# The feed-forward residual and the second activation tile change places, the first output units go by halves, and pads move the small products

## The chip, the cores and the metric

The kernel runs on one core of one Trainium2 chip. The metric is the device time of one execution in microseconds (us); lower is better. Five engines work side by side: TensorE multiplies matrices (PE in the rows), VectorE (DVE), ScalarE (ACT) and GpSimd (POOL) do everything element by element, and SyncE (SP) issues most DMA transfers. Each engine works through its own queue in order and waits on semaphores for the others.

## The reference

One decoder layer on x of 256 positions by 2048 channels, in float32. Two branches run side by side on the normalised x, are weighted by sigmoid gates, added and projected; a convolutional feed-forward block follows. Cut to its core:

```python
h = rmsnorm(x, attn_w)
z, xbc, dt, q, k, v, gates = split(h @ w_in)          # the input projection, in parts
y_ssm  = ssd_mixer(z, xbc, dt, ...) @ w_ssm_out       # 8 groups of 8 heads
y_attn = moba_attention(q, k, v, ...) @ w_attn_out    # 16 heads of 128, with a position bias
g_s, g_a = split(sigmoid(gates + b_gate))
x = x + (g_s * y_ssm + g_a * y_attn) @ w_out
u = causal_dwconv(rmsnorm(x, ffn_w) @ w_up)           # 2 x 5632 channels, 3 taps
out = x + (silu(u[:half]) * u[half:]) @ w_down
```

Inside `ssd_mixer` each group of 512 channels is normalised by the mean of its squares (`yg * rsqrt(mean(yg * yg) + EPS)`). The position bias of a head is a table of 32 buckets, looked up by distance.

## The kernel before

**Tiling.** Activations lie with channels on the 128 partitions and the 256 positions along them. A float32 product is made of three in the rounded format f32r: each operand is split into a high part and a rest, and high x high, high x rest and rest x high are summed. Weights come in units of 1 MB: `unit` loads one into `wraw` (SyncE's queue, three buffers), ScalarE copies each half to `whi` (L181), VectorE forms the rest `wlo` (L182), three buffers each. `cm_chunk` then makes the matmuls of a half: eight pairs of `whi` with high part and rest (L196, L197), eight of `wlo` with the high part (L199), 24 matmuls of 256 columns; a unit has 48. The weights are the stationary operand there, the activations the moving one. In `tm_chunk` (L325, L326, L331: V, Q and K) it is the other way, with 512 columns.

**Stages in time.** V until 126 us; Q, K and attention until 307, then gate and attention output (`hp` and `ot` as moving tiles) until 492; the SSD groups with their input projections (`hn`) and output units (`yt`) until 1246; `w_out` (`mt`) until 1342; the feed-forward block as up and down projections in thirds (`fh` up, `a` down: up 0, up 1, down 0, up 2, down 1, down 2) to the end. The second third's down projection stands at 1908.7 to 2000.8.

**Order.** A scheduler fixes each engine's queue from the order in which the code is written. Attention and SSD steps are lists that `sp.tick()` deals out between the weight units, one step a tick; the steps of an SSD group end with ydot(3), norm1 (squares), norm1b (`all_sum`: split the sum of squares into `nsp`, add over partitions by one matmul with `onesr`, L249) and norm2. In `merge`, each of 16 tiles of the last SSD output units is multiplied by its gate (`gs`) and added to the attention part (`ma`), both loaded by GpSimd (L807, L808), with VectorE's L809 to L811; L812 and L813 write its high part and rest to `mt`, which `w_out` reads.

**Where tiles lie.** The base pool holds the three 32 KB slots of tag s32, `whi`, `wlo` and `wraw`, and stage pools follow behind it. A tile's byte offset in a partition follows from the sizes ahead of it. Offsets modulo 128 in the built program:

| operands of TensorE | offsets before |
|---|---|
| tiles in s32 slots: hp, ot, hn, yt, mt, fh, first and third activation tile | 0 |
| whi, wlo | 64 |
| second activation tile a2 (pool of the feed-forward block) | 64 |
| qh, ql and kh, kl (scores) | 0 and 0 |
| pth, ptl and vt (probabilities by values) | 0 and 0 |
| bch, bcl: first half stationary, second half moving | 96 and 96 |
| xh, xl and mh, ml (ydot) | 96 and 96 |
| nsp, ssp and onesr | 96 and 0 |

## Time and profile before

| | |
|---|---|
| time, median of three runs | 2066.89 us (2066.75 to 2069.88) |
| the profiled execution: time, span | 2071.27 us, 2069.5 us |
| mean granted clock of TensorE | 0.999 of full speed |
| busy: TensorE, VectorE, ScalarE, GpSimd | 99%, 70%, 55%, 3% |
| DMA, mean over the span | 197 GB/s |

The terms of a sum are made from the profiled execution and then set against the median. In rows, a name such as `mm<-hn,whi` reads output, then inputs; a time in square brackets is the idle time before the instruction, with what ended it. Matmuls are pipelined: one of 256 columns is shown as 0.28 us long, while the next starts 0.11 to 0.12 us after it.

### The profile page before, as it was taken

The page shows a single profiled execution, that of the slowest core. Times are in us where ns is not written, and L with a number is a line of the kernel's source. Part 1 is how long each engine was busy: PE and PEld are TensorE (multiplying, and loading weights), DVE is VectorE, ACT ScalarE, POOL GpSimd, SP SyncE. Part 2 cuts the span into 40 slices and gives each one's busy share as a digit, 9 for nine tenths or more (in the row PEclk, how much of TensorE's full clock was granted, in tenths as well). Part 3 has the DMA queues.
Part 4 walks back from the last instruction along what each step waited for, and adds up shares of the span by engine and source line. Part 5 has one row for each costly group of instructions (what it writes and reads, how often), then busy time and mean ns, then how long its engine had stood idle before and what let it go on. Part 6 is the DMA issues. An engine that isn't in the chain of part 4 may idle for free.

```text
span 2069.5 us, 39670 instructions
## 1 busy us (share of the span) xinstructions
PE 2053.5 (99%) x16594; PEld 1995.0 (96%) x16594; DVE 1457.4 (70%) x2324; ACT 1146.9 (55%) x1565; POOL 62.7 (3%) x119
## 2 busy tenths in 40 slices
PE   8999999999999999999999999999999999999999
PEld 7888889999999999999999999999999999999999
DVE  6567777456678787787888786677777765677444
ACT  6456556444557756656566654565555553455333
POOL 0000000000000000000000120000000000000000
PEclk9999999999999999999999999999999999999999
DMA  7654446555555555555555666555555555555555
GB/s 275 249 189 154 172 173 215 195 203 194 205 194 203 195 195 190 178 203 194 186 199 187 217 238 233 190 184 199 189 199 189 200 188 201 187 201 188 183 177 170
DMA packets 65892, 407.45 MB, mean 197 GB/s; under 512 B 8405, under 2 KB 10469, under 8 KB 22192
## 3 DMA queue, kind: packets, MB, share of 16 engines
q1 hardware_dynamic: 55152, 376.45, 51.7%
q0 software_dynamic: 7104, 22.17, 3.4%
q10 hardware_dynamic: 3456, 6.29, 0.9%
q8 instruction: 130, 2.13, 0.4%
q14 instruction: 50, 0.41, 0.1%
HBM read 398.50 MB, written 9.53 MB: 197 GB/s over the span
## 4 chain that ended last, share of the span: by engine, by line
PE 95%; DVE 1%; issue 1%; DMA 1%; ACT 1%; POOL 0%; SPq 0%; POOLq 0%; DVEq 0%
PE mm L197 26%; PE mm L196 26%; PE mm L199 26%; PE mm L325 4%; PE mm L331 4%; PE mm L326 4%; PE cc L210 1%; PE cc L209 1%; PE cc L211 1%; DVE wlo L182 1%; DMA g<-gs 1%; PE cc L418 0%; PE cc L666 0%; DMA g<-ma 0%; DMA wraw<-wv 0%
## 5 line engine op out<-in xcount | busy, mean ns | idle before, releaser
L181 ACT ACTIVATE whi<-wraw 128x1024 fp32r<-128x1024 f32 (+2 forms) x728 | 756.1, 1041 | 767.0 <-PE mm L197 632.6
L182 DVE TENSOR_TENSOR wlo<-wraw,whi 128x1024 fp32r<-128x1024 f32 (+2 forms) x728 | 870.0, 1197 | 313.4 <-ACT whi L181 308.4
L196 PE MATMUL mm<-hn,whi 128*128 128x256 f32 x1536 | 359.7, 277 | 0.0
L197 PE MATMUL mm<-hn,whi 128*128 128x256 f32 x1536 | 358.9, 276 | 0.0
L197 PE MATMUL mm<-fh,whi 128*128 128x256 f32 x1408 | 328.0, 276 | 0.0
L196 PE MATMUL mm<-fh,whi 128*128 128x256 f32 x1408 | 328.0, 276 | 0.0
L196 PEld LDWEIGHTS mm<-hn,whi 128*128 128x128 f32 x1536 | 288.6, 188 | 0.1
L197 PEld LDWEIGHTS mm<-hn,whi 128*128 128x128 f32 x1536 | 288.4, 188 | 0.0
L196 PEld LDWEIGHTS mm<-fh,whi 128*128 128x128 f32 x1408 | 264.3, 188 | 0.0
L197 PEld LDWEIGHTS mm<-fh,whi 128*128 128x128 f32 x1408 | 264.3, 188 | 0.0
L199 PE MATMUL mm<-hn,wlo 128*128 128x256 f32 x1536 | 205.9, 276 | 0.0
L199 PEld LDWEIGHTS mm<-hn,wlo 128*128 128x128 f32 x1536 | 188.6, 188 | 0.0
L199 PE MATMUL mm<-fh,wlo 128*128 128x256 f32 x1408 | 188.3, 276 | 0.0
L199 PEld LDWEIGHTS mm<-fh,wlo 128*128 128x128 f32 x1408 | 172.7, 188 | 0.0
L197 PE MATMUL mm<-a,whi 128*128 128x256 f32 x704 | 167.5, 279 | 0.0
L196 PE MATMUL mm<-a,whi 128*128 128x256 f32 x704 | 167.5, 279 | 0.0
L325 PE MATMUL mm<-whi,hp 128*128 128x512 f32 x384 | 153.6, 400 | 6.8 <-ACT whi L181 6.7
L326 PE MATMUL mm<-whi,hp 128*128 128x512 f32 x384 | 151.8, 395 | 0.0
L197 PEld LDWEIGHTS mm<-a,whi 128*128 128x128 f32 x704 | 133.2, 189 | 0.0
L196 PEld LDWEIGHTS mm<-a,whi 128*128 128x128 f32 x704 | 133.2, 189 | 0.0
L196 PE MATMUL mm<-yt,whi 128*128 128x256 f32 x512 | 119.3, 276 | 0.0
L197 PE MATMUL mm<-yt,whi 128*128 128x256 f32 x512 | 119.3, 276 | 0.0
(290 smaller groups left out, 3182.0 us busy)
## 6 DMA issues: line engine op xcount, KB each, us to landing
wraw<-wup SPq DMA_DIRECT2D x88, 1024.0 KB, 4.8
wraw<-wssd SPq DMA_DIRECT2D x80, 1024.0 KB, 4.8
wraw<-wqk SPq DMA_DIRECT2D x32, 1024.0 KB, 4.8
wraw<-wso SPq DMA_DIRECT2D x32, 1024.0 KB, 4.9
wraw<-wd SPq DMA_DIRECT2D x32, 1024.0 KB, 4.8
wraw<-wga SPq DMA_DIRECT2D x16, 1024.0 KB, 4.9
wraw<-wao SPq DMA_DIRECT2D x16, 1024.0 KB, 5.0
wraw<-wgs SPq DMA_DIRECT2D x16, 1024.0 KB, 4.8
```

The costliest lines, as they stand in the source:

```text
L181: S.activation(hi[:, i:i + m], raw[:, s], AF.Copy)
L182: V.tensor_tensor(lo[:, i:i + m], raw[:, s], hi[:, i:i + m].bitcast(F32), op=SUB)
L196: PE.matmul(ps, w, xh[:, k0 + k], start=first and k == 0, stop=False)
L197: PE.matmul(ps, w, xl[:, k0 + k], start=False, stop=False)
L199: PE.matmul(ps, lo[:, k * 128:(k + 1) * 128], xh[:, k0 + k], start=False, stop=last and k == nk - 1)
L209: PE.matmul(ps, ah, bh, start=first, stop=False)
L210: PE.matmul(ps, ah, bl, start=False, stop=False)
L211: PE.matmul(ps, al, bh, start=False, stop=last)
L325: PE.matmul(pst[tt], hph[:, k0 + k, ts], wh, start=first and k == 0, stop=False)
L326: PE.matmul(pst[tt], hpl[:, k0 + k, ts], wh, start=False, stop=False)
L331: PE.matmul(pst[tt], hph[:, k0 + k, ts], wl, start=False, stop=last and k == 1)
```

## The change

The residual `x1` moves from an s32 slot to a tile of its own in the feed-forward pool, and the second activation tile, which stood in that pool, to the slot; the third activation tile takes the first one's. The first two `w_out` units are multiplied by halves: first half of unit 0, first half of unit 1, second half of 0, second half of 1. The split of the sum of squares moves into the step of ydot(3) and the squares, an empty step follows, and the matmul comes in norm1b as before. The fp32 bias product becomes two f32r products, for which ScalarE and VectorE split the table `rel` and VectorE casts the one-hot table `oh`. Pads (`pad2` to `pad4`, and 16 columns in `bch` and `bcl`) shift tiles.

```diff
@@ -242,9 +242,15 @@
 
 
     def all_sum(pool, v, out, name, **kw):
+        sum_out(sum_split(pool, v, name, **kw), out)
+
+    def sum_split(pool, v, name, **kw):
         t = pool.tile([128, 2, T], F32R, name=name, **kw)
         S.activation(t[:, 0], v, AF.Copy)
         V.tensor_tensor(t[:, 1], v, t[:, 0].bitcast(F32), op=SUB)
+        return t
+
+    def sum_out(t, out):
         ps = c_tile()
         PE.matmul(ps.rearrange("p (a t) -> p a t", t=T), onesr, t, start=True, stop=True)
         S.activation(out, ps[:, T:], AF.Copy)
@@ -306,8 +312,14 @@
         oh = ap.tile([REL_BUCKETS + 1, 384], F32, name="oh")
         nc.gpsimd.dma_start(rel, d["rel"])
         nc.gpsimd.dma_start(oh, d["onehot"])
+        ohr = ap.tile([REL_BUCKETS + 1, 384], F32R, name="ohr")
+        rels = ap.tile([REL_BUCKETS + 1, 2, H], F32R, name="rels")
+        V.tensor_copy(ohr, oh)
+        S.activation(rels[:, 0], rel, AF.Copy)
+        V.tensor_tensor(rels[:, 1], rel, rels[:, 0].bitcast(F32), op=SUB)
         pb = c_tile()
-        PE.matmul(pb[:H, :384], rel, oh, start=True, stop=True)
+        PE.matmul(pb[:H, :384], rels[:, 0], ohr, start=True, stop=False)
+        PE.matmul(pb[:H, :384], rels[:, 1], ohr, start=False, stop=True)
         rows = ap.tile([H, 384], F32, name="brows")
         V.tensor_copy(rows, pb[:H, :384])
         nc.gpsimd.dma_start(brow, rows)
@@ -377,6 +389,7 @@
 
     _, oh_, ol_ = r32("ot")
     pts = []
+    ap.tile([128, 16], F32, name="pad3")
     for i in range(2):
         pth = ap.tile([128, 512], F32R, name=f"pth{i}")
         ptl = ap.tile([128, 512], F32R, name=f"ptl{i}")
@@ -416,6 +429,8 @@
                 for h in range(2):
                     for tt in range(2):
                         PE.transpose(ps[:, h * 256 + tt * 128:h * 256 + (tt + 1) * 128], n[:, tt, 2 * (j % 2) + h], ident)
+                if j == 0 and key == "k":
+                    ap.tile([128, 16], F32, name="pad4")
                 hi = ap.tile([128, 512], F32R, name=key + "h", bufs=1)
                 lo = ap.tile([128, 512], F32R, name=key + "l", bufs=1)
                 S.activation(hi, ps, AF.Copy, scale=w)
@@ -639,8 +654,8 @@
             last = S.activation(pr, pr, AF.Silu)
             with tc.issue_after(last.ins):
                 S.preload_act_table_set(LN_EXP)
-            bh = sd.tile([128, 2, T], F32R, name="bch")
-            bl = sd.tile([128, 2, T], F32R, name="bcl")
+            bh = sd.tile([128, 2, T + 16], F32R, name="bch")[:, :, :T]
+            bl = sd.tile([128, 2, T + 16], F32R, name="bcl")[:, :, :T]
             S.activation(bh, pr[:, 8:10], AF.Copy)
             V.tensor_tensor(bl, pr[:, 8:10], bh.bitcast(F32), op=SUB)
             st["b"] = (bh, bl)
@@ -699,6 +714,8 @@
                 m1 = m[:, 512:768].rearrange("p (h t) -> p h t", t=128)
                 V.tensor_tensor(m0, m0, st["cb"][:, None, 0:256].to_broadcast([128, 2, 256]), op=MUL)
                 V.tensor_tensor(m1, m1, st["cb"][:, None, 256:384].to_broadcast([128, 2, 128]), op=MUL)
+                if g == 0 and p == 0:
+                    sd.tile([128, 16], F32, name="pad2")
                 mh = sd.tile([128, 768], F32R, name="mh", bufs=2)
                 ml = sd.tile([128, 768], F32R, name="ml", bufs=2)
                 S.activation(mh, m, AF.Copy)
@@ -729,11 +746,11 @@
             S.activation(sq2, yz[:, 2:4], AF.Square)
             V.tensor_tensor(sqt, sqt, sq2, op=ADD)
             V.tensor_tensor(sqt[:, 0], sqt[:, 0], sqt[:, 1], op=ADD)
-            st["sq"] = sqt
+            st["sq"] = sum_split(sd, sqt[:, 0], "nsp", tag="cb")
 
         def norm1b():
             w = sd.tile([128, 3, T], F32, name="nw", tag="m", bufs=2)
-            all_sum(sd, st["sq"][:, 0], w[:, 0], "nsp", tag="cb")
+            sum_out(st["sq"], w[:, 0])
             V.tensor_scalar(w[:, 0], w[:, 0], 1.0 / 512, EPS, op0=MUL, op1=ADD)
             st["r"] = rsq_in(w[:, 0], w[:, 1], w[:, 2])
 
@@ -747,8 +764,8 @@
             S.activation(yh, yz, AF.Copy)
             V.tensor_tensor(yt[:, b, 1, o:o + 4], yz, yh.bitcast(F32), op=SUB)
 
-        steps = [silu, [bc, xtr(0), xtr(1)], dec(0), dec(1), ydot(0), dec(2), ydot(1), dec(3), ydot(2), ydot(3),
-                 norm1, norm1b, norm2]
+        steps = [silu, [bc, xtr(0), xtr(1)], dec(0), dec(1), ydot(0), dec(2), ydot(1), dec(3), ydot(2), [ydot(3), norm1],
+                 [], norm1b, norm2]
         return steps
 
     def out_unit(q, u, done):
@@ -819,14 +836,22 @@
 
     fctx = contextlib.ExitStack()
     fp = fctx.enter_context(tc.tile_pool(name="ffn", bufs=1))
-    x1f = xs_slot("x1")
-    x1 = x1f[:, :KT * T].rearrange("p (k t) -> p k t", t=T)
+    x1 = fp.tile([128, KT, T], F32, name="x1")
     for c in range(4):
         S.dma_start(x1[:, 4 * c:4 * c + 4], d["xT"][:, 4 * c:4 * c + 4])
     _, fh, fl = r32("fh")
     ssum = fp.tile([128, T], F32, name="ssum")
-    for o in range(KT):
-        ps = cm_unit(d["wout"][o], mh_, ml_)
+
+    def out_products():
+        parts = [unit(d["wout"][o]) for o in range(2)]
+        pss = [mm_tile()[:, :T] for _ in range(2)]
+        for c in range(2):
+            for o in range(2):
+                cm_chunk(pss[o], parts[o][c], mh_, ml_, 8 * c, 8, c == 0, c == 1)
+        for o in range(KT):
+            yield o, pss[o] if o < 2 else cm_unit(d["wout"][o], mh_, ml_)
+
+    for o, ps in out_products():
         V.tensor_tensor(x1[:, o], ps, x1[:, o], op=ADD)
         S.activation(fh[:, o], x1[:, o], AF.Copy, scale=sm("ffn_w", o))
         V.scalar_tensor_tensor(fl[:, o], x1[:, o], sm("ffn_w", o), fh[:, o].bitcast(F32), op0=MUL, op1=SUB)
@@ -847,8 +872,8 @@
 
     def up(th):
         f0, n = thirds[th]
-        if th == 1:
-            at = fp.tile([128, 2, 16, T], F32R, name="a2")
+        if th == 2:
+            at = acts[0]
         else:
             at = base.tile([128, 2, 16, T], F32R, name=f"a{th}", tag="s32", bufs=3)
         for i in range(n):
```

Offsets modulo 128 that differ in the built program: second activation tile 0 (weights still 64), qh and ql 64 (kh, kl 0), pth and ptl 64 (vt 0), bch and bcl 96 stationary and 32 moving, mh and ml 32 (xh, xl 96). The other operands of the table keep theirs.

On TensorE, at the start of `w_out`, last rests of the halves; `mm` is the output unit, `wlo` the half. Before:

```order
L199 MATMUL mm_14256<-mt_13610,wlo_14249 128x256 x8
...
L199 MATMUL mm_14256<-mt_13610,wlo_14253 128x256 x8
...
L199 MATMUL mm_14319<-mt_13610,wlo_14312 128x256 x8
...
L199 MATMUL mm_14319<-mt_13610,wlo_14316 128x256 x8
L196 MATMUL mm_14384<-mt_13610,whi_14376 128x256
```

With the change:

```order
L199 MATMUL mm_14275<-mt_13619,wlo_14258 128x256 x8
...
L199 MATMUL mm_14276<-mt_13619,wlo_14268 128x256 x8
...
L199 MATMUL mm_14275<-mt_13619,wlo_14262 128x256 x8
...
L199 MATMUL mm_14276<-mt_13619,wlo_14272 128x256 x8
L196 MATMUL mm_14393<-mt_13619,whi_14385 128x256
```

The second unit's first half now stands ahead of the first unit's second half, the first that reads late tiles of `mt`; units from the third on stand as before.

On VectorE, at the end of the merge (`slotA` is the sum, `g` the gates and the merged tile). Before:

```order
L811 TENSOR_TENSOR g<-slotA,g 128x256
L809 TENSOR_TENSOR slotA<-mm,slotA 128x256
L182 TENSOR_TENSOR wlo<-wraw,whi 128x1024
L813 TENSOR_TENSOR mt<-g,mt 128x256
L810 TENSOR_TENSOR slotA<-slotA,g 128x256
L811 TENSOR_TENSOR g<-slotA,g 128x256
L813 TENSOR_TENSOR mt<-g,mt 128x256
L830 TENSOR_TENSOR x_14239<-mm,x_14239 128x256
```

With the change (L826, L827, L828 and L830 are what L809, L810, L811 and L813 were; L855 is the addition to x):

```order
L828 TENSOR_TENSOR g<-slotA,g 128x256
L826 TENSOR_TENSOR slotA<-mm,slotA 128x256
L182 TENSOR_TENSOR wlo<-wraw,whi 128x1024
L830 TENSOR_TENSOR mt<-g,mt 128x256
L827 TENSOR_TENSOR slotA<-slotA,g 128x256
L828 TENSOR_TENSOR g<-slotA,g 128x256
L182 TENSOR_TENSOR wlo<-wraw,whi 128x1024
L830 TENSOR_TENSOR mt<-g,mt 128x256
L182 TENSOR_TENSOR wlo<-wraw,whi 128x1024
```

One more weight rest stands ahead of the last tile's rest, and one behind it; the weight rest behind the first gate addition shown is still behind it.

On ScalarE, at the end of SSD group 0 (`pre` and silu are group 1's, `sqt` the squares, L774 a gate of the SSD branch). Before:

```order
L639 ACTIVATE pre_4836<-pre_4836 128x2560
L774 ACT_TABLE_LOAD
L774 ACTIVATE g<-mm,small 128x256
L729 ACTIVATE sqt_6346<-slotA 128x512
L181 ACTIVATE whi<-wraw 128x1024 x2
L246 ACTIVATE nsp<-sqt_6345 128x256
```

With the change:

```order
L654 ACTIVATE pre_4844<-pre_4844 128x2560
L746 ACTIVATE sqt_6293<-slotA 128x512
L791 ACT_TABLE_LOAD
L791 ACTIVATE g<-mm,small 128x256
L249 ACTIVATE nsp<-sqt_6292 128x256
L181 ACTIVATE whi<-wraw 128x1024 x3
```

The squares go ahead of the table load and the gate, and the copy into `nsp` ahead of two weight halves. On VectorE the rest of `nsp` follows the sum of the squares in the same way, and on TensorE the matmul with `onesr` stands eleven matmuls earlier in groups 0 and 1, in the same place in groups 2 and 3.

## Rows read from the trace of the kernel before

**Rows 1.** The page: busy time of each engine, share of the span, instructions.

```profile
PE 2053.5 (99%) x16594; PEld 1995.0 (96%) x16594; DVE 1457.4 (70%) x2324; ACT 1146.9 (55%) x1565; POOL 62.7 (3%) x119
```

**Rows 2.** Stretches: us, TensorE busy (count), granted clock, DMA share, GB/s.

```profile
62.00:125.00 63.00, 63.00 (x277) 1.00 0.67 245
334.20:518.70 184.50, 184.50 (x1569) 1.00 0.59 208
520.00:545.00 25.00, 25.00 (x223) 1.00 0.69 240
1255.40:1258.60 3.20, 3.20 (x17) 0.50 0.78 275
1259.00:1343.00 84.00, 84.00 (x716) 1.00 0.55 194
1691.20:1777.00 85.80, 85.80 (x759) 1.00 0.54 196
1910.00:2000.00 90.00, 90.00 (x752) 1.00 0.50 176
```

**Rows 3.** Timeline of TensorE, end of attention: start, busy us, line, operands.

```profile
333.39 0.28 PE L209 MATMUL cc<-pth,vt 128*128 128x256 f32 x1
...
333.99 0.28 PE L211 MATMUL cc<-pth,vt 128*128 128x256 f32 x1
```

**Rows 4.** Waits of TensorE: total us, times, longest.

```profile
PE cc L249 <- DVE nsp L247: 2.8, 4, 0.7
```

**Rows 5.** Timeline of TensorE around nsp, group 0.

```profile
622.84 0.28 PE L196 MATMUL mm<-hn,whi 128*128 128x256 f32 x1
...
624.94 0.47 PE L249 MATMUL cc<-nsp,onesr 128*128 128x512 f32 x1 [0.69 <-DVE nsp L247]
625.25 0.28 PE L197 MATMUL mm<-hn,whi 128*128 128x256 f32 x1
```

**Rows 6.** Timeline of ScalarE ahead of it.

```profile
620.38 0.62 ACT L729 ACTIVATE sqt<-slotA 128x512 f32<-128x512 f32 x1
...
622.80 0.41 ACT L246 ACTIVATE nsp<-sqt 128x256 fp32r<-128x256 f32 x1
```

**Rows 7.** Timeline of VectorE ahead of it.

```profile
624.38 0.42 DVE L247 TENSOR_TENSOR nsp<-sqt,nsp 128x256 fp32r<-128x256 f32 x1
```

**Rows 8.** Timeline of TensorE, start of the output projection.

```profile
1250.25 0.28 PE L197 MATMUL mm<-mt,whi 128*128 128x256 f32 x1
1251.59 0.38 PE L196 MATMUL mm<-mt,whi 128*128 128x256 f32 x1 [1.06 <-ACT mt L812]
1252.94 0.38 PE L197 MATMUL mm<-mt,whi 128*128 128x256 f32 x1 [0.97 <-DVE mt L813]
1254.18 0.38 PE L196 MATMUL mm<-mt,whi 128*128 128x256 f32 x1 [0.86 <-ACT mt L812]
...
1258.87 0.28 PE L197 MATMUL mm<-mt,whi 128*128 128x256 f32 x1
```

**Rows 9.** Timeline of VectorE, end of the merge.

```profile
1250.66 0.42 DVE L811 TENSOR_TENSOR g<-slotA,g 128x256 f32<-128x256 f32 x1 [1.51 <-DMA g<-ma]
...
1251.34 1.21 DVE L182 TENSOR_TENSOR wlo<-wraw,whi 128x1024 fp32r<-128x1024 f32 x1
```

**Rows 10.** Timeline of GpSimd: issues of the one-hot table and of the attention gate.

```profile
2.00 0.54 POOL L308 DMA_DIRECT2D oh<-onehot  x1
...
1243.87 0.54 POOL L808 DMA_DIRECT2D g<-ma  x1 [0.74 <-DVE slotA L810]
```

**Rows 11.** The page's DMA issues: count, KB each, median us to landing.

```profile
g<-ma POOLq DMA_DIRECT2D x16, 128.0 KB, 4.4
...
oh<-onehot POOLq DMA_DIRECT2D x1, 49.5 KB, 4.3
```

**Rows 12.** Timeline of TensorE, bias product.

```profile
60.10 0.81 PE L310 MATMUL cc<-oh,rel 33*16 33x384 f32 x2
```

**Rows 13.** Timeline of VectorE, first hp rests.

```profile
4.70 0.88 DVE L256 SCALAR_TENSOR_TENSOR hp<-xt,aw,hp 128x256 fp32r<-128x256 f32 x2 [4.70 <-ACT hp L255]
```

## The prediction

> **What bounds the kernel now.** I read the busy table first: TensorE is busy for 2053.5 of 2069.5 us [rows 1]. The waits of TensorE come next: past the one ahead of the first matmul they are a handful, so removing waits alone can give little. The third view cuts the busy time by stage [rows 2], and that is where this change can act. The count of a stretch takes in two matmuls that lap over its ends, so the starts are the count less two, and the stretch divided by them is the **step** from one matmul to the next. All matmuls of 256 columns do the same work, and yet the step has three values at full clock: 113.1 and 113.3 ns in the SSD stage (25.00 us / 221) and for the first activation tile (85.80 / 757), 117.7 and 117.6 ns in the gates and the attention output (184.50 / 1567) and in the output projection (84.00 / 714), and 120.0 ns for the second activation tile a2 (90.00 / 750). The reader is to see that a busy TensorE is not the same as a fast one: between the levels lie 4.5 and 6.7 ns for every matmul.
>
> What separates the levels I read by laying addresses beside steps. Where the two operands of a matmul lie at the same byte offset modulo 128 (a2 and its weights, both 64), the step is 120.0. The products of probabilities and values (both 0) step by (333.99 - 333.39) / 5 = 0.120 us too [rows 3]. Where they differ by 64 (all activation tiles of the base slots, 0, against weights at 64) it is 113 or 117.7. The level 117.7 has no operands of its own: it holds for tiles that elsewhere run at 113, is there from 334.2 on, right behind those products, and lasts through ot, hp and hn; hn's matmuls alone, from 520 on, are at 113.1 again. I read it as a slower phase that a stretch of same-offset matmuls or a stall leaves behind, and that lasts until something resets it. The 120.0 is shown directly; the phase is my inference.
>
> **The change part by part**, against the profiled 2071.3 us (span 2069.5).
>
> *a) Second activation tile in a base slot.* Its offset goes from 64 to 0, against weights at 64, as the first tile has it. Sixteen units of 48 matmuls = 768, by 120.0 - 113.3 = 6.7 ns: **-5.1 us**. Lower gain: if the tile lands in the 117.7 phase, 768 x 2.3 ns = 1.8. The exchange costs nothing else: x, now in the pool, is no operand of TensorE; the last third takes up the first tile's memory again, which the down projection before it has finished reading.
>
> *b) The pads in the attention stage.* They move pth/ptl to 64 (vt stays 0) and qh/ql to 64 (kh/kl stay 0). Their 192 matmuls of 256 columns lose 192 x 6.7 ns = 1.3 us directly. The 512-column units between them may sit in the same phase: seven groups of 24 after such products, by some 4 ns (an estimate, from the 4.5 above), is 0.7. With the hidden-state units at the end of the stage 2.2; bounds 0.5 and 3.5: **-2.2**. If no same-offset products stand before 334.2, the phase isn't entered there and 1567 matmuls return to 113.2: 1567 x 4.5 ns = **-7.0**; if it is entered for another reason, 0.
>
> *c) The pads in the SSD stage.* bch/bcl now pair 96 with 32, mh/ml 32 with xh/xl 96. These are 96 + 48 matmuls of 256 columns by at most 6.7 ns and 96 of 512, which I bound by the same: 0 to 1.6, taken as **-1.0**. This is below the middle of what 192 such matmuls cost in b) because the stream runs at 113.1 around them.
>
> *d) Group norm.* Four waits of TensorE for nsp, 2.8 us in all [rows 4]; each costs more than its idle time, since the matmul before it and after it drain and refill: in group 0 it starts 624.94 - 622.84 = 2.10 us after the chunk's first matmul, where the eleven ahead of it need 11 x 0.113 = 1.25, and the next follows 0.31 later where a 512-column step is 63.00 us / 275 = 0.229 [rows 2, 5]. So 0.85 + 0.08 = 0.93, four times 3.7. Now nsp's copy and rest stand in the step of the squares: on ScalarE the squares go ahead of a table load and a gate that stood ahead of them, so all three end where the squares end today, 620.38 + 0.62 = 621.00; the copy follows at once, 0.41 [rows 6], and on VectorE the rest, 0.42 [rows 7]: ready at about 621.9. Its matmul moves eleven earlier, to the start of the chunk at 622.84 [rows 5]: 0.9 us of slack. Behind the copy on ScalarE the next weight halves come some 0.4 us later, and no wait of TensorE for them exists around here to grow. **-3.7**, bounds 2 and 3.7.
>
> *e) First output units by halves.* TensorE runs dry here because the last two merged tiles, high part and rest, come late: waits until 1251.59, 1252.94 and 1254.18, then 15 matmuls in 3.20 us (213 ns) at granted clock 0.50, that is the lower level, 1.2 GHz [rows 2, 8]. The 26 matmuls between 1250.25 and 1258.87 took 8.6 us where 26 x 113.3 ns = 2.95 would do; 5.7 are lost. The cause is a transfer: VectorE's addition waits 1.51 us for the attention gate until 1250.66 [rows 9]; issued at 1243.87 [rows 10], it took 6.8 us against a median of 4.4 [rows 11]. Now TensorE does both units' first halves first, which need no late tile: 48 matmuls from 1246.29, done by 1251.7. But the second unit's first half needs its wlo from VectorE, which stands behind that very addition: at 1251.34 + 1.21 = 1252.55 it is there, while its matmuls are due at 1250.82. The wait is not gone, it **moved**: at most 1.7 us, and 0.15 when the transfer takes its usual time. The last tile's rest now stands behind one more wlo, at about 1255.1, 0.15 late at most. Units one and two end at about 1258.8 instead of 1263.0: **-4.2**. What follows, some 700 matmuls at 117.6, entered the phase by the stall at the lower clock; with one stall of 1.7 us in place of three and no lower clock I expect 113: 700 x 4.4 ns = **-3.1**, else 0. x's transfer is issued earlier on ScalarE's queue, between two weight halves, and waits for nothing recent: 0.
>
> *f) Bias product.* Two passes in fp32, busy 0.81 us [rows 12], become two of 384 columns; at 0.229 for 512, 0.17 each: **-0.4**.
>
> *g) The start.* The split of rel and the cast of the one-hot table now stand first on VectorE. The table is issued at 2.00 [rows 10] and lands 4.3 us later [rows 11], so the first hp rest comes at about 7.2 instead of 4.70 + 0.44 [rows 13], just where TensorE wants it, 7.25. Everything on VectorE behind it, the first wlo too, waits along. The weights' arrival paces TensorE there. **+0.1**, bounds 0 and 0.4.
>
> Sum: -5.1 - 2.2 - 7.0 - 1.0 - 3.7 - 4.2 - 3.1 - 0.4 + 0.1 = **-26.6**, hence 2044.7 profiled. The profiled execution stands 4.4 us above the median of 2066.9 (runs to 2069.9); part of that may be the same late transfer, so I take 25 off the median: **2042**, main band 2037 to 2046.
>
> **The rivals.** *R1, the phase stays* from 334 to 519: something else than the same-offset products starts it. For it: it also begins behind the stalls after 1251 [rows 2, 8]. Against: the products right ahead of its start step by 120 [rows 3]. b) gives 7.0 less: **2049**. With e)'s phase staying as well, 2052.
>
> *R2, placement does nothing:* the steps differ for what runs beside the matmuls, not for addresses. Then only d), e) without the phase, f) and g) remain: 8.2 of 2066.9, **2059**. Against it: the second tile's matmuls are the same as the first's, beside less traffic (DMA share 0.50 against 0.54 [rows 2]), and slower. The Trainium skill would side with R2: its page "SBUF — State Buffer", section "Who interferes with whom", gives TensorE two independent read ports for moving operand and weights and says that it never waits on anyone; the trace speaks against that, with 120.0 and 113.3 ns for the same shapes.
>
> *R3, slower:* the small products at their new offsets leave the phase behind in the SSD stage, which today is free of it: mh with xh at equal offsets are followed by 113.1 [rows 2]. From 519 to 1246 there are some 6,400 matmuls: 6,400 x 4.5 ns = 28.4 us back, and if the gates' 7.0 isn't won either, 2042 + 35.4 = **2077**. It decides from where 25 us are lost: without the gates' 7.0, when 4,000 of the 6,400 run at 117.6. Against it: a2 shows the price of equal offsets, and no long stretch with a difference of 64 that begins from 113 leaves it by itself.
>
> **How the numbers follow.** Forecast 0.63; R1 (with or without the output projection) 0.15; R2 0.08; R3 0.06; partial mixtures between 2052 and 2066 0.08. The range 2036 to 2054 holds the first two and the lower mixtures. What can be told from no change here is about 0.2%, 4.1 us: faster (below 2062.8) takes all but R3 and a little of the mixtures, 0.91; R3 where it is partial ends within, 0.04; slower 0.05.
>
> **What would show it.** Right: the second tile's stretch at 113.3 per step; 334 to 487 at 113; no wait for nsp; one wait for wlo of at most 1.7 us in the second output unit's first half and a granted clock of 1.00 there; the stretch behind it at 113. Wrong: 117.6 in the SSD stage or in the gates, or a2's successor at 120.0, which would refute the reading by offsets. A longer start would show in the first wait of hp's rest.

## The result

The changed kernel takes 2054.61 us (median of four runs, 2052.70 to 2058.32) where the kernel before takes 2067.5: a ratio of 0.9938, interval 0.992 to 0.9956. A later set gave 2054.23 (nine runs) and 0.9924, 0.9891 to 0.9958. The forecast was 2042, range 2036 to 2054: right in sign, about half of it in size. The runs of one kernel fall in two groups some 20 to 30 us apart, both at full granted clock, the kernel before at 2064.7 to 2073.6 (105 of 134 runs over all sets) and 2087.3 to 2096.3 (29), which widens the intervals and turned out to be part of the subject.

The profiled execution of the changed kernel took 2052.70 us, span 2050.9. By stages, from the first matmul of one to the first of the next, in the two traces (518 is where two small transposes open the SSD groups):

| stage | before, us | after, us | change | forecast |
|---|---|---|---|---|
| start to first matmul on ot | 334.11 | 333.36 | -0.8 | -2.5 (b directly, f, g) |
| gates and attention output, to 518 | 184.68 | 184.68 | 0.0 | -7.0 (b, phase) |
| SSD, to the first matmul on mt | 727.50 | 723.72 | -3.8 | -4.7 (c, d) |
| output projection | 95.84 | 87.04 | -8.8 | -7.3 (e) |
| up 0 to up 2 | 566.6 | 566.5 | -0.1 | 0 |
| down 1, down 2 | 160.8 | 155.6 | -5.2 | -5.1 (a) |
| sum | 2069.5 | 2050.9 | -18.6 | -26.6 |

The page after, busy time of each engine:

```profile
PE 2040.6 (99%) x16594; PEld 1983.6 (97%) x16594; DVE 1457.0 (71%) x2326; ACT 1146.2 (56%) x1566; POOL 62.5 (3%) x119
```

The stretches that answer to [rows 2] (us, TensorE busy with the count, granted clock, DMA share, GB/s; the starts are the count less two):

```profile
334.00:518.00 184.00, 184.00 (x1564) 1.00 0.58 208
520.00:545.00 25.00, 25.00 (x223) 1.00 0.65 226
1244.00:1328.00 84.00, 84.00 (x743) 1.00 0.57 201
1678.00:1764.00 86.00, 86.00 (x761) 1.00 0.55 196
1896.00:1985.00 89.00, 89.00 (x788) 1.00 0.53 189
```

The second activation tile, the last line, steps by 89.00 / 786 = 113.2 ns where it took 120.0. The output projection, third line, runs at 84.00 / 741 = 113.4 instead of 117.6. The second, hn, and the fourth, the first activation tile, are as before. The first line is the miss: 184.00 / 1562 = 117.8, as before.

TensorE's waits and its timeline at the end of attention:

```profile
PE mm L337 <- ACT whi L181: 6.7, 1, 6.7
PE cc L255 <- PE mm L196: 0.2, 1, 0.2
```

```profile
331.94 0.28 PE L209 MATMUL cc<-pth,vt 128*128 128x256 f32 x1
...
332.65 0.28 PE L209 MATMUL cc<-pth,vt 128*128 128x256 f32 x1
...
333.24 0.28 PE L211 MATMUL cc<-pth,vt 128*128 128x256 f32 x1
333.36 0.28 PE L196 MATMUL mm<-ot,whi 128*128 128x256 f32 x1
```

No wait for nsp is left [rows 4]; the 0.2 us are at the sum of squares ahead of the feed-forward block, ssp, which the same helper makes. The products of probabilities and values now have their operands 64 bytes apart modulo 128, and they step by (333.24 - 332.65) / 5 = 0.118 us, where I expected 0.113. All twelve do, from 331.94 to 333.36, and ot goes on at 0.118.

TensorE and VectorE at the group norm of group 0, in answer to [rows 5] and [rows 7]:

```profile
622.08 0.39 PE L255 MATMUL cc<-nsp,onesr 128*128 128x512 f32 x1
622.32 0.28 PE L196 MATMUL mm<-hn,whi 128*128 128x256 f32 x1
```

```profile
620.58 0.42 DVE L250 TENSOR_TENSOR nsp<-sqt,nsp 128x256 fp32r<-128x256 f32 x1 [0.94 <-ACT nsp L249]
```

nsp is complete at 621.00 and wanted at 622.08: one microsecond of slack, close to the 0.9 of the forecast.

### The profile page after: what moved, and what is told of

Its sections match the earlier page's. It is cut to its first block, busy times and chain, and to the rows that moved or that the text cites. A ratio compares the mean times of both kernels' runs of the same rounds, so it can differ in the third digit from the quotient of the medians.

```text
span 2050.9 us, 39668 instructions
## 1 busy us (share of the span) xinstructions
PE 2040.6 (99%) x16594; PEld 1983.6 (97%) x16594; DVE 1457.0 (71%) x2326; ACT 1146.2 (56%) x1566; POOL 62.5 (3%) x119
## 4 chain that ended last, share of the span: by engine, by line
PE 99%; DMA 0%; DVE 0%; ACT 0%; SPq 0%; issue 0%
PE mm L196 27%; PE mm L199 27%; PE mm L197 27%; PE mm L337 4%; PE mm L343 4%; PE mm L338 4%; PE cc L209 1%; PE cc L211 1%; PE cc L210 1%; PE cc L431 0%; PE cc L681 0%; DMA wraw<-wv 0%; ACT whi L181 0%; PE cc L255 0%; DVE wlo L182 0%; PE cc L475 0%
## 5 line engine op out<-in xcount | busy, mean ns | idle before, releaser
L196 PE MATMUL mm<-a,whi 128*128 128x256 f32 x704 | 164.3, 276 | 0.0
L197 PE MATMUL mm<-a,whi 128*128 128x256 f32 x704 | 164.3, 276 | 0.0
```

The lines of the kernel that those rows point to most:

```text
L196: PE.matmul(ps, w, xh[:, k0 + k], start=first and k == 0, stop=False)
L197: PE.matmul(ps, w, xl[:, k0 + k], start=False, stop=False)
```

## Experiments

The theory going in was that of the prediction: equal offsets cost 6.7 ns a matmul, and a slow phase of 117.7 ns, once entered, lasts until something resets it. I call the two levels, 113.3 and 117.7, rhythms from here on: the fast and the slow one. The rivals: something else than equal offsets starts the slow phase (R1), the stage itself for instance, or placement does nothing (R2). Medians are compared within the lower group of each kernel, against the kernel before on the same chip; its median is 2067 to 2069.5 in every set.

### Placement of the second activation tile alone

Both on the kernel before, a pad ahead of a2, of 64 bytes and of 1984:

```diff
+            fp.tile([128, 16], F32, name="pad5")
             at = fp.tile([128, 2, 16, T], F32R, name="a2")
```

> The kernel before with one tile of 64 bytes put ahead of the second activation tile a2 in the feed-forward pool, so that a2 begins at offset 0 modulo 128 instead of 64; nothing else changes. Theory (equal offsets modulo 128 of moving operand and weights cost 6.7 ns a matmul): a2's matmuls step by 113.3 ns instead of 120.0, 768 x 6.7 ns = 5.1 us less, ratio about 0.9975. Rival (the tile is slow for what runs beside it, or because it lies in the pool): still 120.0, ratio 1.000.

> The kernel before with 1984 bytes ahead of the second activation tile in the pool, so that its offset agrees with that of the slots modulo 2048 and not only modulo 128. Theory (a pass from one moving tile to another whose offset agrees further than modulo 128 is no break, one that agrees modulo 128 alone is): a2 steps by 113.3 where the stream ahead of it does, 5.1 us less than before in such runs. Rival (only the base slots do, or the rhythm at that place is picked at random): 117.8, as with 64 bytes.

The stretch of the second tile with 64 bytes, then with 1984:

```profile
1910.00:1990.00 80.00, 80.00 (x682) 1.00 0.53 187
```

```profile
1910.00:1990.00 80.00, 80.00 (x709) 1.00 0.54 188
```

With 64 bytes the step is 80.00 / 680 = 117.6 ns, with 1984 it is 80.00 / 707 = 113.2. With 1984 bytes the runs agree: 2062.5 (eleven runs, none high) against 2067.3, the 5 us of the forecast. With 64 bytes the step is worth 768 x 2.4 ns = 1.8 us, which the runs can't show: 2069.2 against 2069.5 (lower groups, each spread over 3 to 5 us; six of twelve runs were high, ten of 29 of the kernel before beside them). R2 falls: nothing but an address moved. The Trainium skill, page "SBUF — State Buffer", section "Who interferes with whom", gives TensorE independent read ports for the moving operand and the weights and has it never wait on anyone. By that rule the step would not have changed, and here it went from 120.0 to 113.2. But my rule was too coarse: with 64 bytes neither its 113.3 nor the rival's 120.0 came. Modulo 512, the moving offset less that of the weights is 0 for a2 as it was (120.0), 64 with the first pad (117.6), 448 with the second and for all slots.

### The gates: is it a rhythm left behind?

On the changed kernel, behind the last product of probabilities and values:

```diff
     sp.flush()
+    rp = c_tile()
+    for i in range(2):
+        PE.transpose(rp[:, i * 128:(i + 1) * 128], ident, ident)
     attn.close()
```

> The changed kernel with two 128 x 128 transposes of the identity put on TensorE right behind the last product of probabilities and values, ahead of the first matmul on ot. Theory (the level of 117.7 ns is a phase that those products leave behind and that lasts until something resets it; transposes do): the stretch from 334 to 519 us steps by 113.3, about 1567 x 4.5 ns = 7.0 us less, less 0.3 to 0.4 for the transposes and the refill: 2054.6 - 6.6 = 2048. Rival (this stage is slow by its own operands or traffic): 117.7 there as before, 2055.

```profile
334.00:354.00 20.00, 20.00 (x178) 1.00 0.72 241
360.00:511.00 151.00, 151.00 (x1335) 1.00 0.60 211
```

```profile
357.92 0.50 PE L199 MATMUL mm<-hp,wlo 128*128 128x256 f32 x2 [1.03 <-DVE wlo L182]
```

The same matmuls and operands, beside like traffic, step by 151.00 / 1333 = 113.3 behind two transposes. The span is 2045.6; in three of six runs the time is 2046.4 to 2049.0. So the stage does not make the slow rhythm: it comes with those products and stays behind them, whatever their offsets. That form of R1 is left. Why transposes should end it, the kernel before could have told: at the end of its slow stretch, in [rows 2], stand two of its own, with no wait.

```profile
518.79 0.38 PE L614 MATMUL cc<-small,slotA 128*128 128x128 f32 x2
```

Two of the six runs were at 2054 and 2055 and one at 2077.5. No profile shows them; the next sections give what I take for their cause. The third line of this section, a wait of 1.03 us for wlo, is where the first two may begin: at the faster step TensorE now meets VectorE, which prepares hn in this stretch.

Next, whether the order of operands matters: vt in the odd half, pth in the even one, as in the stream:

```diff
-    vt = base.tile([128, 2, 2, DM], F32R, name="vt", tag="s32", bufs=3)
+    vt = base.tile([128, 8224], F32R, name="vt", tag="s32", bufs=3)[:, 16:8208]
+    vt = vt.rearrange("p (a b c) -> p a b c", a=2, b=2)
...
-    ap.tile([128, 16], F32, name="pad3")
...
+                if j == 0 and key == "q":
+                    ap.tile([128, 16], F32, name="pad6")
```

> The changed kernel with vt at offset 64 modulo 128 and pth, ptl at 0, so that in the products of probabilities and values the moving operand has the even half and the weights the odd one, as in the weight units around them, instead of the reverse; q stays at 64 and k at 0. Theory (the products leave the phase behind because their operands lie the other way round than the stream's): these products step by 113.3 and the stretch behind them, 334 to 519 us, too: 7.0 and up to 0.5 us less, 2047 to 2048. Rival (any group of foreign products leaves it, whichever way round): they step by 117.7 and so does the stretch, 2054 to 2055.

```profile
340.00:495.00 155.00, 155.00 (x1319) 1.00 0.59 206
530.00:555.00 25.00, 25.00 (x223) 1.00 0.67 232
1360.00:1680.00 320.00, 320.00 (x2720) 1.00 0.53 188
```

The gates stay at 117.7, as the rival had it, and 1360 to 1680 runs at 320.00 / 2718 = 117.7: ten of twelve runs lay at 2094 to 2099. The edit was no clean test. Longer slots moved them apart: ot, yt and fh now stand at a difference of 64 modulo 512 to the weights, hn, mt and the second activation tile at 192, hp and the first at 320; hn, second line, still runs at 25.00 / 221 = 113.1. What it showed instead was a whole feed-forward stage in the slow rhythm, and the size of the upper group. The two other runs, at 2072.5 and 2074.6, are some 24 us lower. The tiles that don't stand at 64 could give 19 at most (some 4,300 slow matmuls by 4.4 ns), so tiles at 64 must have run faster in them, which no profile shows.

### Where the upper group comes from

The changed kernel again; then with transposes behind the last product and behind ssp; then the kernel before with transposes behind ssp alone, twice:

```diff
     all_sum(fp, ssum, ssum, "ssp")
+    restart()          # two transposes, as above
```

> The changed kernel once more, beside many runs of the kernel before. Theory (the long stream of matmuls has two rhythms, 113.3 and 117.8 ns, and a break in it, a stall or a foreign matmul, picks one that then holds until the next break; the last break ahead of the feed-forward stream is the matmul that sums the squares, ssp): most runs at 2053 to 2058, and some about 28 us above (6,300 matmuls x 4.5 ns), where the kernel before has some about 22 us above its low ones, since its second activation tile steps by 120.0 either way. Rival (the high runs are another disturbance, the same for both kernels): the high runs of the two stand equally far above their low ones.

> The changed kernel with two transposes of the identity behind the last product of probabilities and values and two more right behind the matmul of ssp. Theory (rhythm picked at the break at ssp): no runs some 28 us above the others; all within 2045 to 2053, median 2048. Rival (the high runs come from something else): one to five in twelve still at 2075 or more.

> The kernel before with two transposes of the identity right behind the matmul of ssp and nothing else. Theory (rhythm picked at ssp): its runs at 2091 to 2096 vanish, all lie at 2067 to 2074. Rival (another disturbance): about a third of its runs still at 2091 to 2096, as without the transposes.

> The kernel before with the two transposes behind ssp once more, for one profile, since 8 of its 12 runs lay at 2088 to 2093. Theory (the high runs are the slow rhythm through the feed-forward stage): if this execution is a high one, the stretches on fh and the first activation tile step by 117.8 and the rest as in low ones; it shows where the rhythm changes. Rival (high runs are spread over all stages or come from the granted clock): steps of 113.3 there and the time elsewhere.

The changed kernel had no high run in its 13, which bears out neither side. Transposes at ssp did not help: four of twelve high (2076 to 2082), and on the kernel before eight of twelve, more than without (nine of 33 on the same chip). The second time this kernel's profile is of a high execution, 2089.84 us. Its stretches, and below them one of a low execution of the same kernel, 2073.28:

```profile
1290.00:1338.00 48.00, 48.00 (x426) 1.00 0.54 196
1350.00:1690.00 340.00, 340.00 (x2889) 1.00 0.53 187
1930.00:2010.00 80.00, 80.00 (x669) 1.00 0.51 178
2020.00:2080.00 60.00, 60.00 (x532) 1.00 0.60 197
```

```profile
1360.00:1690.00 330.00, 330.00 (x2914) 1.00 0.54 196
```

Ahead of ssp 48.00 / 424 = 113.2, behind it 340.00 / 2887 = 117.8, at the same granted clock, until a2 at 119.9; behind a2 113.2 again. The low execution has 330.00 / 2912 = 113.3 in the same place.

```profile
1342.77 0.28 PE L196 MATMUL mm<-fh,whi 128*128 128x256 f32 x1
1343.29 0.47 PE L254 MATMUL cc<-ssp,onesr 128*128 128x512 f32 x1 [0.24 <-PE mm L196]
```

So this high execution has the slow rhythm, taken up at ssp, where TensorE stands still (0.52 us to the next start), and held for 580 us. Some 4,900 matmuls by 4.5 ns are 22 us, the distance of the groups. For the upper groups elsewhere it is inferred from that size. That is a part of "the phase" that the prediction had not seen: the same standstill gives either rhythm, from one execution to the next.

### A standstill, or any break?

The matmul of ssp behind the first two up units instead of inside the first, so that TensorE does not wait for it, on the changed kernel with the transposes after attention, and on the kernel before:

```diff
-    all_sum(fp, ssum, ssum, "ssp")
+    ssp = sum_split(fp, ssum, "ssp")
+    ahead = [cm_unit(d["wup"][t], fh, fl) for t in (0, NFF)]
+    sum_out(ssp, ssum)
```

> The changed kernel with the two transposes behind the last product of probabilities and values, and with the matmul of ssp behind the first two up units instead of inside the first, so that TensorE doesn't stand still for it. Theory (at a break where TensorE stands still, the rhythm behind it falls at random from run to run; at a break without a wait it is the same in every run): no wait ahead of ssp, and the feed-forward stage takes the same rhythm in every run: no run some 28 us above the others if it is 113.3, all within 2045 to 2053. Rival (random at any break): some of twelve runs still at 2075 or more.

> The kernel before with the matmul of ssp behind the first two up units and nothing else. Theory (the standstill at ssp makes the rhythm fall at random): the runs at 2087 to 2096, some 3 in 10 before, vanish or become all; if the rhythm kept is 113.3, all lie at 2065 to 2072; mt's slow phase then reaches the first two up units, 0.4 us. Rival (random at any break): about 3 in 10 still high.

All twelve runs of the one at 2073 to 2085 and all six of the other at 2087 to 2095, beside 20 of 23 runs of the kernel before at 2066 to 2071. Without the standstill the rhythm behind ssp was, by these times, the same in every run, and it was the slow one. The edit also moves ssp from inside a pair of matmuls on the same weights to between two units; no run parts the two. A third kernel had a sixth gate buffer besides (`bufs=6`):

> The kernel with the late ssp and the transposes, and a sixth buffer for the gates, so that the loads of the merge are issued half a merge earlier. Theory (the low runs of the changed kernel spread over 2052 to 2058 because the second output unit's weights wait behind a late load): its runs lie closer together, within 3 us, and its median 1 to 3 us under the kernel with five buffers. Rival (the spread is that of the start and of the weights' own transfers): the same spread and median within 1 us.

2075.1 against 2075.0, the same spread, as the rival had it: the gate loads are not what spreads the runs. Its trace shows both kinds of break:

```profile
334.00:354.00 20.00, 20.00 (x179) 1.00 0.72 237
360.00:516.00 156.00, 156.00 (x1327) 1.00 0.57 204
1300.00:1328.00 28.00, 28.00 (x250) 1.00 0.53 189
1350.00:1650.00 300.00, 300.00 (x2550) 1.00 0.52 187
```

```profile
357.52 0.86 PE L199 MATMUL mm<-hp,wlo 128*128 128x256 f32 x5 [1.00 <-DVE wlo L182]
```

```profile
1338.52 1.07 PE L199 MATMUL mm<-fh,wlo 128*128 128x256 f32 x8
1339.42 0.39 PE L255 MATMUL cc<-ssp,onesr 128*128 128x512 f32 x1
```

Ahead of the wait for wlo at 357.52 the step is 20.00 / 177 = 113.0, behind it 156.00 / 1325 = 117.7. In the execution of the kernel with transposes shown above, the same wait left 113.3 behind. At ssp, which here follows eight matmuls in 0.90 us without a wait, 28.00 / 248 = 112.9 turns into 300.00 / 2548 = 117.7.

If transposes without a standstill set the fast rhythm, they must stand behind the late ssp. They also stand behind the last product of probabilities and values, the sixth attention output unit (which comes after the wait for wlo) and the first two output units:

> The changed kernel with the matmul of ssp behind the first two up units and two transposes of the identity at four places: behind the last product of probabilities and values, behind the sixth attention output unit, behind the first two output units, and right behind the matmul of ssp. Theory (at a break without a standstill the rhythm is the same in every run, and transposes leave 113.3): the stream is at 113.3 from each of the four places on, no run lies some 28 us high, all twelve lie within 2045 to 2051, median 2047. Rival (transposes leave either rhythm, as the profile of the kernel before with transposes at ssp seems to say, and not the standstill there decides): some runs at 2073 or more.

> The kernel with the late ssp and transposes at four places once more, for more runs. Theory (rhythm the same in every run behind transposes without a standstill): all within 2045 to 2051. Rival: one or more at 2073 or above.

```profile
380.00:512.00 132.00, 132.00 (x1167) 1.00 0.56 202
1260.00:1322.00 62.00, 62.00 (x549) 1.00 0.56 197
1340.00:1660.00 320.00, 320.00 (x2826) 1.00 0.55 195
```

All ten runs at 2046.7 to 2050.1, none high; 113.3, 113.3 and 113.3 ns per step. The medians are 2047.8 and 2048.5, ratio 0.9905 (0.9888 to 0.9921) in the first set, where neither kernel had a high run: 19 us under the kernel before and 6 under the changed one. This is the version that beats both.

> The kernel before with the late ssp, the same four pairs of transposes, and 1984 bytes ahead of a2; without the halves, the early split of the sums, the pads and the f32r bias product. Theory (most of the changed kernel's gain is the rhythm): 2067 less 5.1 for a2, less 5 to 7 for the gates, less 0 to 3 for mt, 2052 to 2057, no runs 20 us above. What it stands above the kernel with both, 2048, is then what the waits for nsp (3.7) and the halves (1 to 5) are worth by themselves. Rival (the halves and the norm carry the gain): 2060 or more.

The same four pairs, the late ssp and the 1984 bytes on the kernel before: 2058.3, twelve runs at 2055 to 2064, none high, between the 2052 to 2057 expected and the rival's 2060. 2067.8 - 2058.3 = 9.5 us are the rhythm's and a2's alone. It could be more: in the profile a wait of 0.4 us for weights right behind the transposes leaves mt in the slow rhythm, 3 us. The 10 us from there to 2048.3 hold these 3 and the change's halves, norm, bias product and early x; they were not priced one by one on this kernel.

### The halves, and the merge's loads

The output units in their old order, on the changed kernel:

```diff
-    for o, ps in out_products():
+    for o in range(KT):
+        ps = cm_unit(d["wout"][o], mh_, ml_)
```

> The changed kernel with the output units from the first on in the order of the kernel before, each unit's two halves behind one another; all else as changed. Theory (the halves are what takes the waits for the last merged tiles and the low clock away): TensorE waits again for mt about 1251, the 768 matmuls on mt take 4 to 9 us longer, low runs at 2058 to 2063. Rival (the pads and the earlier transfer of x do it): as the changed kernel, 2052 to 2058.

```profile
1246.02 0.38 PE L196 MATMUL mm<-mt,whi 128*128 128x256 f32 x1 [0.29 <-ACT mt L829]
1247.38 0.39 PE L197 MATMUL mm<-mt,whi 128*128 128x256 f32 x1 [0.97 <-DVE mt L830]
1248.62 0.58 PE L196 MATMUL mm<-mt,whi 128*128 128x256 f32 x1 [0.86 <-ACT mt L829]
1249.64 0.58 PE L197 MATMUL mm<-mt,whi 128*128 128x256 f32 x1 [0.44 <-DVE mt L830]
```

```profile
1246.00:1254.00 8.00, 5.71 (x23) 0.66 0.65 248
1275.00:1335.00 60.00, 60.00 (x532) 1.00 0.55 194
```

The waits for mt are back, with a mean granted clock of 0.66 in those 8 us. The lower group is at 2057.4 against 2054.2 to 2054.6 with the halves (on other chips, whose kernel before agrees within 0.5): 3 us, where 4 to 9 were expected. Behind these standstills the stream ran at 60.00 / 530 = 113.2 here, and at 117.6 in the profile of before: either rhythm again.

The attention part of the merge in buffers of its own:

```diff
-        a = gate_pool.tile([128, T], F32, name="g", bufs=5)
+        a = sd.tile([128, T], F32, name="mg", tag="xf" if o % 2 else "m", bufs=2)
```

> The changed kernel with the attention part of the merge loaded into buffers of its own (in tiles of the SSD pool that are idle by then), so that both loads of a merge are issued earlier, by one or two merges. Theory (the runs of the changed kernel that are 3.5 to 5.5 us above its fastest are those in which a load of the merge comes late and stalls the first output units, with the slow phase behind it): the runs fall together within 1 us of 2052.7 and no VectorE wait for such a load shows. Rival (the spread has another source): runs still spread over 4 to 6 us, median 2054 to 2055.

```profile
PE mm L196 <- ACT whi L181: 2.6, 1, 2.6
```

```profile
1252.26 0.42 DVE L855 TENSOR_TENSOR x<-mm,x 128x256 f32<-128x256 f32 x1 [6.63 <-DMA x<-xT]
```

2054.4 to 2059.0 in the lower group, and four of twelve runs high at 2082 to 2085: no better, as the rival had it. In its trace x's transfers are issued at 1245.7 instead of 1193.0 to 1197.5, I take it because the new tiles lie where x is loaded. VectorE's first addition on x then waits 6.63 us, ScalarE has work on its result ahead of the next weight half, and TensorE waits 2.6 us for that. It shows what the move of x into the pool brought unnoticed: x is issued some 50 us ahead of its first use.

### Offsets of the whole stream

`pad1` longer by 256 and by 32 bytes, on the changed kernel:

```diff
-    base.tile([128, 16], F32, name="pad1")
+    base.tile([128, 80], F32, name="pad1")      # and [128, 24]
```

> The changed kernel with pad1 256 bytes longer, so that the weight halves begin 320 instead of 64 behind the slots' offset modulo 512 (moving minus weights: 192 instead of 448). Theory (which rhythms the stream can have is set by this difference modulo 512: 0 and 128 give 120.0, 64 gives 117.8, 448 either of 113.3 and 117.8): at 192 the steps of the long stretches take another pattern than in the changed kernel, either 113.3 throughout, gates included, 2046 to 2049 without runs some 28 us above, or 117.8 throughout, 2085 to 2090. Rival (only modulo 128 counts): 117.7 in the gates, 113.3 elsewhere, and a median of 2054 as in the changed kernel.

> The changed kernel with pad1 32 bytes longer, so that the weight halves begin at 96 instead of 64 (moving minus weights 416 instead of 448 modulo 512). Theory (rhythms set by the difference modulo 512): one of the two levels throughout, or a new one; if 113.3 throughout, 2046 to 2049 and no runs some 28 us above. Rival (only halves of 128 bytes count, 96 lies in the same half as 64): as the changed kernel, 117.7 in the gates, 2052 to 2058.

```profile
340.00:490.00 150.00, 150.00 (x1276) 1.00 0.58 203
1360.00:1670.00 310.00, 310.00 (x2738) 1.00 0.54 194
```

```profile
340.00:495.00 155.00, 155.00 (x1323) 1.00 0.59 207
1360.00:1680.00 320.00, 319.87 (x2724) 1.00 0.53 188
```

At a difference of 192 all is as at 448, 150.00 / 1274 = 117.7 and 310.00 / 2736 = 113.3, median 2053.9, so that the rival was right about this one. At 416 there is no fast rhythm: 117 to 119 ns throughout, 2115.5 us, 2.3% slower than before (1.0228, 1.0192 to 1.0263) for 32 bytes; neither side had that.

Modulo 512 is more than the runs show. 192 and 448 agree modulo 256, and so do the differences with one and the same step elsewhere: 0 (a2) and 256 (the products of probabilities and values before) at 120.0, 64 and 320 (ot and hp in the first line of the odd vt) at 117.7. No run has a difference of 128, which the expectation names.

## Why the prediction was half right

**a) Right, -5.2 for -5.1.** The step fell from 120.0 to 113.2 for the placement. The reason given, a difference of 64 modulo 128, is not enough: with 64 bytes of pad the same tile ran at 117.6. What carried it is that the tile now lies as the first one does, which a) says too.

**b) The step that failed**, in its words: "If no same-offset products stand before 334.2, the phase isn't entered there". The pads did part the offsets, and the products fell from 120 to 118 ns, worth 0.4 us by 192 x 2.2 ns, but the stretch behind them stayed at 117.8. That it is a rhythm left behind was right, as transposes show; that equal offsets start it was wrong: at 256, 448, 64 and 192 (before, after, odd vt, offset 192) the products were followed by the slow one alike. The trace of before speaks against it too. There the products of the scores, both operands at 0, step by (321.11 - 319.67) / 12 = 0.120 us, and hp behind them by (323.83 - 321.11) / 24 = 0.113:

```profile
319.67 0.28 PE L209 MATMUL cc<-kh,qh 128*128 128x256 f32 x1
...
321.11 0.28 PE L196 MATMUL mm<-hp,whi 128*128 128x256 f32 x1
...
323.83 0.28 PE L196 MATMUL mm<-hp,whi 128*128 128x256 f32 x1
```

So some products leave the slow rhythm and others the fast one; why, no run tells. R1 had the outcome here and gave 2049. The small products gained some 0.4 and not 2.2, since those of probabilities and values only came down to the slow step.

**c) Wrong, about 0 for -1.0.** The six products of mh and xh at offsets 32 and 96 take 1.05 us (579.74 to 580.79 in the trace of after), at 96 and 96 they took 1.04 (580.50 to 581.54). That leaves the stage's 3.8 us to nsp.

**d) Right**, all four waits gone.

**e) Right in kind, in the profile larger than forecast**, -8.8 for -7.3: the wait for wlo that was to be at most 1.7 us did not come in this execution; a second profile of the kernel has it with 0.6 us. But this term was made from an execution of the kernel before with an unusually bad passage, 4.4 us above its median. I set 25 of 26.6 us off the median, where the median runs had less to lose here: no_halves prices the halves at 3 us. This is the second step that failed, worth about 4 us: the term that was mis-sized is the 4.2 + 3.1 = 7.3 of the halves, which measured 3.

**f), g) Right, near enough**: from the bias product to the next matmul it is 60.77 - 60.33 = 0.44 us instead of 60.84 - 60.10 = 0.74, so -0.3 for -0.4; the first hp rest begins at 6.43, behind the cast, and no wait follows.

```profile
6.15 0.35 DVE L317 CAST ohr<-oh 33x384 fp32r<-33x384 f32 x1 [0.61 <-DMA oh<-onehot]
6.43 0.86 DVE L262 SCALAR_TENSOR_TENSOR hp<-xt,aw,hp 128x256 fp32r<-128x256 f32 x2
```

```profile
60.33 0.34 PE L321 MATMUL cc<-ohr,rels 33*16 33x384 f32 x1
60.52 0.33 PE L322 MATMUL cc<-ohr,rels 33*16 33x384 f32 x1
```

Together: 7.0 short at the gates and 2.6 at the small products, less 1.6 at e) and a), are the 8.0 between -26.6 and -18.6; the other 4.6 of the 12.6 between 2042 and 2054.6 are the basis. Two slips in the working changed nothing: in R3, 6,400 x 4.5 ns is 28.8 and not 28.4 us, and in e) the wait of 1.7 us less the 1.51 that VectorE waits is 0.2 and not 0.15.

**R3**, the slow rhythm in long stretches, was put at 6% and in the wrong place, the SSD stage. It exists in the feed-forward stage, by their times in 29 of 134 runs of the kernel before; in the changed kernel it would cost about 28 us (late_ssp: 2075.0, less 2047 to 2048), but none of its 13 runs had it. Whether that is chance stays open: of kernels with the same ssp, no_halves and offset_192 had one high run in ten each, ma_early four in twelve.

Open too is what in the memory makes the levels. The runs show at which differences of offset 113.3 was seen, and which breaks were followed by which rhythm, not why. Nor do they show why the transposes set the fast one only where TensorE had not just stood still.

## What to carry to other kernels

Where TensorE is busy throughout, divide stretches by their counts before looking for waits: a step a few per cent too long over thousands of matmuls was worth more than every wait in the profile. If a level depends on what came before, put a cheap break ahead of the long stretch, away from any standstill, and see whether the level follows. Make a term that rests on one rare passage from the median run, not from the execution that happened to be profiled.

## What the runs showed of the hardware

- A stream of 256-column matmuls in f32r ran at 113.3 or 117.8 ns per step, at the same granted clock and with the same operands. A level, once taken, held over thousands of matmuls and changes of tile.
- The difference of the moving operand's and the weights' byte offset modulo 512 set what was seen: 192 and 448 either level, 64 and 320 117.7 in every profile, 0 and 256 120.0, 416 117 to 119. Whether 64 allows 113.3 too is open, as two runs of the odd vt suggest.
- A break without a standstill was followed by the same level in every run, as their times and six profiles tell it (the late ssp: slow in 30 of 30; transposes behind it: fast in 22 of 22). A standstill of TensorE was followed by either (ssp, and the wait for wlo at 357).
